# Opening a fused encoder step with three plain feed-forward tiles instead of four, and with token-wise sums of squares

## Chip, cores, metric

The kernel runs on one core of one Trainium2 chip. The metric is the device time of one execution in microseconds, given as the median of several runs. A profile is one further execution, recorded by the hardware profiler.

## What is computed

One inference step of an encoder trunk with two layers, for 512 prompt frames and 8 x 16 sample frames, 640 tokens in all, width 1024. Each layer has a half-step feed-forward block, a mixer (short convolution, banded attention, gates) and a second half-step feed-forward block. What matters here is the very first feed-forward block:

```python
def _rmsnorm(x, g):
    xf = x.astype(jnp.float32)
    y = xf * lax.rsqrt(jnp.mean(xf * xf, axis=-1, keepdims=True) + EPS)
    return y.astype(x.dtype) * g

def _swiglu(h, w_gu, w_down):
    gu = h @ w_gu
    g, u = jnp.split(gu, 2, axis=-1)
    return (jax.nn.silu(g) * u) @ w_down
...
xp = xp + 0.5 * _swiglu(_rmsnorm(xp, norm_ffn1[l]), w_ffn1_gu[l], w_ffn1_down[l])
```

The inner width is 2816, that is 22 tiles of 128 columns for the gate and 22 for the up projection.

## The kernel before

**Layout and precision.** Activations lie transposed: 128 channels on the partitions, 640 tokens along the row, eight such k-tiles `x[0..7]`, each in two halves of 320 tokens. Every operand of a matrix product is split into a high part (`hi`, a rounded copy made by ScalarE, `ACT`) and a low part (`lo`, source minus high part, made by VectorE, `DVE`). A product is the sum of three matmuls: high by high, high by low, low by high. Weights stream from HBM as slabs of 128x1024 (`raw`), and each slab is split the same way (`whi` at L305, `wlo` at L310).

**Plain tiles and tiles by seven.** A plain gate or up product of one 128-column tile takes 8 k-tiles x 3 x 2 halves = 48 matmuls of 320 columns. A pair of gate and up takes two such products, 96 matmuls. The alternative computes gate and up together by a seven-product scheme of the Strassen kind over halves of k (even and odd k-tiles), halves of tokens and the pair gate/up: seven blocks of 12 matmuls, 84 in all. The blocks are named by their left operand: X11, XT5, XN6, X21, XT7, X22, XT4, in the order of the first such tile. This scheme needs sums of x (`Expand`, with the pieces `xe` of an even row and `xo` of an odd row, held split as `xhi`/`xlo`, four pairs of rows), and sums of weights: four slabs per tile, made out of two raw slabs by VectorE additions at L249 (`s`, then `raw<-raw,raw` and `raw<-s,raw`).

**The opening (`opening`, before the first tile by seven).** The sums of x are not there yet when the kernel starts, so the first tiles of the block are plain. `FFNS["a0"]` says how many: 4. Their eight products `po` 0 to 7 alternate gate and up. They run on x times the gain only; the rms factor per token (`rho`) is applied afterwards, when a product is taken out of its bank. The two banks of `po` alternate, so product i+2 needs product i taken out. Sums of squares come from ScalarE squares (L571, L574), VectorE additions into `ssum`, a matmul with a column of ones (`nps`, L472), a square root on ScalarE, a reciprocal and a diagonal on VectorE, and two matmuls that spread the factor over the partitions (`nbc`, L595), which ScalarE copies into `rho` (L597). Then the first tile by seven is computed by `gate_up` with `first` set; its third block may start only when ScalarE has copied the first block's sum out of the same bank (`c1`, L761).

**Order.** In this part PE, DVE and ACT issue in the order of the code (`manual_schedule`), each engine its own queue. Where one instruction waits, everything behind it on that engine waits. SP issues the loads of x and the slabs, three slab buffers deep. After the opening come tile 4, and then, in turn, two down products (`pd`, taken into x at L1102) and one tile by seven.

## Time and profile before

| | before |
|---|---|
| median of 3 runs | 2496.51 us (2495.89 to 2498.94) |
| the profiled execution | 2496.66 us |
| its span from first to last instruction | 2494.7 us |
| PE, DVE, ACT busy | 99%, 85%, 58% of the span |
| PE matmuls | 17048 |
| moved by DMA | 308.10 MB |
| granted clock of TensorE | 0.998 |

In the rows below, a line begins with the start in microseconds from the span's start and its length, then engine, source line, operation, result and sources, the shape, how many were merged, and in brackets how long the engine had been idle and what ended that. In the chain rows stand start, length, engine and result. In the rows by stretch stand the stretch, its length, the busy time and count of PE, PE's weight loads, DVE, ACT and POOL, then granted clock, DMA share and GB/s. Lengths overlap slightly on one engine, so the price of an operation is better read from start to start.

### The profile page before, as it was taken

The page shows a single profiled execution, that of the slowest core. Times are in us where ns is not written, and L with a number is a line of the kernel's source. Part 1 is how long each engine was busy: PE and PEld are TensorE (multiplying, and loading weights), DVE is VectorE, ACT ScalarE, POOL GpSimd, SP SyncE. Part 2 cuts the span into 40 slices and gives each one's busy share as a digit, 9 for nine tenths or more (in the row PEclk, how much of TensorE's full clock was granted, in tenths as well). Part 3 has the DMA queues.
Part 4 walks back from the last instruction along what each step waited for, and adds up shares of the span by engine and source line. Part 5 has one row for each costly group of instructions (what it writes and reads, how often), then busy time and mean ns, then how long its engine had stood idle before and what let it go on. Part 6 is the DMA issues. An engine that isn't in the chain of part 4 may idle for free.

```text
span 2494.7 us, 43515 instructions
## 1 busy us (share of the span) xinstructions
PE 2478.1 (99%) x17048; PEld 2419.0 (97%) x17048; DVE 2119.2 (85%) x3322; ACT 1450.0 (58%) x2343; POOL 370.7 (15%) x445
## 2 busy tenths in 40 slices
PE   9999999999999999999999999999999999999998
PEld 8999999888999999999999999998899999999998
DVE  7888888878888899888798889888788888989887
ACT  7455556674666555555565555556646665555554
POOL 0011211211111011111001111221111110111111
PEclk9999999999999999999999999999999999999999
DMA  4245665335345344655435555643344553455554
GB/s 146 82 107 124 138 135 130 106 115 167 99 119 145 101 116 118 138 135 135 117 90 126 129 134 123 138 119 115 125 153 104 126 141 95 119 133 122 129 135 110
DMA packets 133261, 308.10 MB, mean 124 GB/s; under 512 B 12768, under 2 KB 76128, under 8 KB 133056
## 3 DMA queue, kind: packets, MB, share of 16 engines
q1 hardware_dynamic: 68976, 219.18, 27.3%
q0 software_dynamic: 63360, 85.50, 20.6%
q8 instruction: 133, 2.18, 0.4%
q10 hardware_dynamic: 720, 0.65, 0.1%
q14 instruction: 72, 0.59, 0.1%
HBM read 221.13 MB, written 7.94 MB: 92 GB/s over the span
## 4 chain that ended last, share of the span: by engine, by line
PE 94%; DVE 3%; ACT 2%; DMA 1%; issue 0%; SPq 0%; DVEq 0%; ACTq 0%
PE pab L395 12%; PE paa L395 11%; PE pcb L395 6%; PE pca L395 6%; PE daa L962 5%; PE dab L962 5%; PE po L372 4%; PE qa L395 4%; PE pbb L395 3%; PE pba L395 3%; PE dca L962 3%; PE dcb L962 3%; PE pda L372 2%; PE pv L1622 2%; PE ma_cv L395 2%; PE qc L395 2%
## 5 line engine op out<-in xcount | busy, mean ns | idle before, releaser
L310 DVE TENSOR_TENSOR wlo<-raw,whi 128x512 fp32r<-128x512 f32 (+1 forms) x583 | 598.6, 1030 | 236.1 <-ACT whi L305 230.6
L305 ACT CAST whi<-raw 128x512 fp32r<-128x512 f32 (+1 forms) x583 | 519.9, 897 | 348.0 <-PE pbb L395 44.6
L305 ACT CAST whi<-s 128x1024 fp32r<-128x1024 f32 (+1 forms) x164 | 153.6, 937 | 248.1 <-issue 107.8
L395 PE MATMUL pab<-xhib,whi 128*128 128x320 f32 x704 | 218.3, 310 | 0.4 <-DVE gb L249 0.4
L395 PE MATMUL pab<-xhib,wlo 128*128 128x320 f32 x704 | 217.4, 309 | 0.0
L395 PE MATMUL pab<-xlob,whi 128*128 128x320 f32 x704 | 217.4, 309 | 0.0
L395 PE MATMUL paa<-xhia,whi 128*128 128x320 f32 x640 | 198.0, 309 | 0.2 <-DVE ga L249 0.2
L395 PE MATMUL paa<-xloa,whi 128*128 128x320 f32 x640 | 197.6, 309 | 0.0
L395 PE MATMUL paa<-xhia,wlo 128*128 128x320 f32 x640 | 197.6, 309 | 0.0
L310 DVE TENSOR_TENSOR wlo<-s,whi 128x1024 fp32r<-128x1024 f32 (+1 forms) x164 | 176.6, 1077 | 10.4 <-ACT whi L305 10.4
L395 PEld LDWEIGHTS pab<-xhib,whi 128*128 128x128 f32 x704 | 132.2, 188 | 1.1 <-DVE gb L249 0.9
L395 PEld LDWEIGHTS pab<-xlob,whi 128*128 128x128 f32 x704 | 132.2, 188 | 0.2
L395 PEld LDWEIGHTS pab<-xhib,wlo 128*128 128x128 f32 x704 | 132.2, 188 | 0.0
L395 PEld LDWEIGHTS paa<-xhia,whi 128*128 128x128 f32 x640 | 120.2, 188 | 0.5 <-DVE ga L249 0.5
L395 PEld LDWEIGHTS paa<-xloa,whi 128*128 128x128 f32 x640 | 120.2, 188 | 0.1
L395 PEld LDWEIGHTS paa<-xhia,wlo 128*128 128x128 f32 x640 | 120.2, 188 | 0.0
L249 DVE TENSOR_TENSOR raw<-raw,raw 128x512 f32<-128x512 f32 x164 | 112.2, 684 | 1.8 <-DMA raw<-in_wst 0.2
L249 DVE TENSOR_TENSOR raw<-s,raw 128x512 f32<-128x512 f32 x164 | 112.3, 685 | 0.0
L395 PE MATMUL pcb<-xhib,whi 128*128 128x320 f32 x352 | 108.7, 309 | 0.0
L395 PE MATMUL pcb<-xlob,whi 128*128 128x320 f32 x352 | 108.7, 309 | 0.0
L395 PE MATMUL pcb<-xhib,wlo 128*128 128x320 f32 x352 | 108.7, 309 | 0.0
L986 POOL DMA_DIRECT2D x<-c_b x52 | 62.6, 1203 | 309.5 <-ACT c_b L979 134.5
(816 smaller groups left out, 8170.8 us busy)
## 6 DMA issues: line engine op xcount, KB each, us to landing
raw<-in_wst SPq DMA_DIRECT2D x375, 512.0 KB, 3.7
x<-c_b POOLq DMA_DIRECT2D x52, 320.0 KB, 5.1
x<-c_a POOLq DMA_DIRECT2D x50, 320.0 KB, 5.0
kc<-in_kcache SPq DMA_DIRECT2D x32, 256.0 KB, 4.1
vc<-in_vcache SPq DMA_DIRECT2D x16, 512.0 KB, 4.5
ub<-cbb POOLq DMA_DIRECT2D x42, 160.0 KB, 5.9
ua<-cba POOLq DMA_DIRECT2D x38, 160.0 KB, 5.4
x<-u_a POOLq DMA_DIRECT2D x18, 320.0 KB, 5.1
```

What stands on the lines that cost most here:

```text
L249: DVE.tensor_tensor(out=out, in0=a, in1=b, op=ALU.add)
L305: ACT.copy(hi[:, d], src[:, c])
L310: DVE.tensor_tensor(out=lo, in0=src, in1=hi.bitcast(F32), op=ALU.subtract)
L372: PE.matmul(ps[a] if isinstance(ps, list) else ps[:, a, :HT], w, x[:, a * HT : (a + 1) * HT], start=first and j == 0, stop=last and j == 2)
L395: PE.matmul(ps, a, b, start=start and kp == 0 and j == 0, stop=stop and kp == NP - 1 and j == 2, skip_group_check=True)
L962: PE.matmul(ps[u], w, y, start=start and i == 0 and j == 0, stop=i == 1 and j == 2, skip_group_check=True)
L986: POOL.dma_start(rows(r, cols), z, accum_op=ALU.add)
L1622: PE.matmul(pv[t], xx[:, t * P : (t + 1) * P], w[:, kk * AW : (kk + 1) * AW], start=c == 0 and kk == 0 and j == 0, stop=c == KT // 2 - 1 a ...
```

## The change

Three plain tiles instead of four, the fourth (tile 3) by seven, so the opening has six products. The first two products are computed side by side, k-tile by k-tile, and the first two slabs are loaded in alternating quarters. For odd rows the operand of the plain products is written where the seven-product scheme wants it, so `Expand.final` no longer casts and splits it a second time. The sums of squares come from a second copy of x laid out by tokens (`xtok`, 5 tiles of 128 tokens x 1024, 2.6 MB), loaded behind x: ScalarE squares each tile in place and sums along the row (`accum_out`). The VectorE additions and the matmul with ones are gone. The tokens lie in buffers that are free at that time.

```diff
-FFNS = {"a0": ((4, 4, 4, 4, 4, 2), 4), "b0": ((4, 4, 4, 4, 6), 0),
+FFNS = {"a0": ((4, 4, 4, 4, 4, 2), 3), "b0": ((4, 4, 4, 4, 6), 0),
...
         if k % 2 == 0:
             c = slice(k * P, (k + 2) * P)
-            SP.dma_start(raws[0][:, c], wst[0][:, c])
+            for n in range(2):
+                SP.dma_start(raws[n][:, c], wst[n][:, c])
...
                 self.flush()
-                ACT.copy(hi[:, 3:5], O[:, 3:5])
+                if whole:
+                    ACT.copy(hi[:, 3:5], O[:, 3:5])
...
-                self.late.append((lo[:, 3:5], O[:, 3:5], hi[:, 3:5]))
+                if whole:
+                    self.late.append((lo[:, 3:5], O[:, 3:5], hi[:, 3:5]))
...
+        ex.ps = fp.tile([P, NT], F32, name=f"sums{name}", bufs=1)
+        load(2)
+        for c in range(NT):
+            if c < 2:
+                z = fp.tile([P, D], F32, tag=("s65", "odd")[c], name=f"tok{name}_{c}", bufs=1)
...
+                SP.dma_start(t, xtok[c][:, a * D // 2 : (a + 1) * D // 2])
...
-        made = {2: (0, 1), 3: (2, 3), 4: (4,), 5: (5, 6), 6: (7,)}
+        made = {2: (2, 3), 3: (4,), 4: (5, 6), 5: (7,)}
...
-        at = {2: {4: begun}, 3: {1: lambda: ex.spread([att(f"nbc{name}_{a}")[:, :HT] for a in range(2)])}}
+        def square(c):
+            for z, total in toks[c]:
+                ACT.activation(z, z, AF.Square, accum_out=total)
+
+        at = {3: {5: lambda: ex.spread([att(f"nbc{name}_{a}")[:, :HT] for a in range(2)])}}
...
             if i == 1:
-                continue
+                ws = [[tiles.take() for _ in range(KT)]]
+                pair = quiet()
+                ws.append([tuple(z[:, k * P : (k + 1) * P] for z in pair) for k in range(KT)])
+                for ks in (*((k,) for k in range(KT - 2)), (KT - 2, KT - 1)):
+                    for p, w in zip(ps, ws):
+                        for k in ks:
+                            multiply(p, w[k], h[k], k == 0, k == KT - 1)
+                flush()
+                ex.final(0, False)
+                square(0)
+                out(0)
+                square(1)
+                ex.final(1, False, True)
+                out(1)
+                square(2)
+                ex.rest()
+                prep(len(ready))
+                flush()
+                for c in range(3, NT):
+                    square(c)
+                add(ex.ps[:, 2:], ex.ps[:, 2:], rest)
+                ex.root()
+                ex.diagonal()
```

What this does to the order is shown at three places. First PE at the start of the program. Before, product 0 (`poa_0`) alone:

```order
L372 MATMUL poa_0_159<-hhia_0_119,whi_117 128x320 x2
L372 MATMUL poa_0_159<-hloa_0_120,whi_117 128x320 x2
L372 MATMUL poa_0_159<-hhia_0_119,wlo_118 128x320 x2
L372 MATMUL poa_0_159<-hhia_1_125,whi_117 128x320 x2
L372 MATMUL poa_0_159<-hloa_1_126,whi_117 128x320 x2
```

Now, the same place on PE; `poa_1` is product 1, and the odd row's operand is `xhia`/`xloa`:

```order
L372 MATMUL poa_0_194<-hhia_0_148,whi_142 128x320 x2
L372 MATMUL poa_0_194<-hloa_0_149,whi_142 128x320 x2
L372 MATMUL poa_0_194<-hhia_0_148,wlo_143 128x320 x2
L372 MATMUL poa_1_195<-hhia_0_148,whi_144 128x320 x2
L372 MATMUL poa_1_195<-hloa_0_149,whi_144 128x320 x2
L372 MATMUL poa_1_195<-hhia_0_148,wlo_145 128x320 x2
L372 MATMUL poa_0_194<-xhia_0_146,whi_142 128x320 x2
```

Product 1's matmuls of a k-tile now follow product 0's of the same k-tile. Second, ACT between the end of product 0 and the square root (`nrmsa`), before; `sqa` are squares of x by channels, `whi` casts of slabs:

```order
L639 COPY ga_0_223<-poa_0_159 128x640
L574 ACTIVATE sqa_2_225<-x 128x640
L574 ACTIVATE sqa_3_228<-x 128x640
L574 ACTIVATE sqa_4_231<-x 128x640
L574 ACTIVATE sqa_5_235<-x 128x640
L574 ACTIVATE sqa_6_238<-x 128x640
L574 ACTIVATE sqa_7_241<-x 128x640
L305 CAST whi_247<-raw_245 128x1024
L305 CAST whi_302<-raw_300 128x1024
L585 ACT_TABLE_LOAD
L585 ACTIVATE nrmsa_113<-npsa_329,epst 128x5
```

And ACT now, on the second half of the way to the root; `toka` are token tiles, squared in place, `xoa` and `xhia` pieces of the first pair of rows:

```order
L677 COPY ua_0_310<-poa_1_195 128x640
L681 ACTIVATE toka_20_130,sumsa_122<-toka_20_130 128x512
L681 ACTIVATE toka_21_132,resta_125<-toka_21_132 128x512
L551 CAST xhia_0_146<-xoa_0_304 128x960
L305 CAST whi_317<-raw_315 128x1024
L681 ACTIVATE toka_30_134,sumsa_122<-toka_30_134 128x512
L681 ACTIVATE toka_31_136,resta_125<-toka_31_136 128x512
L681 ACTIVATE toka_40_138,sumsa_122<-toka_40_138 128x512
L681 ACTIVATE toka_41_140,resta_125<-toka_41_140 128x512
L594 ACT_TABLE_LOAD
L594 ACTIVATE nrmsa_118<-sumsa_122,epst 128x5
```

The root now stands directly behind the squares on the same engine, and the first pair's pieces have moved ahead of it. Third, DVE ahead of the first tile by seven, before; `xoa_3`/`xloa_3` belong to the last pair of rows, `s_8` and `raw_605` are the sums of that tile's weights, `ga_3` the gate of the last plain tile:

```order
L537 TENSOR_TENSOR xoa_3_662<-xoa_3_662,xea_3_597 128x320
L556 TENSOR_TENSOR xloa_3_599<-xoa_3_662,xhia_3_598 128x640
L556 TENSOR_TENSOR xloa_3_599<-xoa_3_662,xhia_3_598 128x960
L249 TENSOR_TENSOR s_8_675<-raw_673 128x512
L249 TENSOR_TENSOR s_8_675<-s_8_675,raw_605 128x512
L487 TENSOR_TENSOR ga_3_729<-poa_6_604,rhoa_116 128x640
L310 TENSOR_TENSOR wlo_679<-s_8_675,whi_678 128x1024
L249 TENSOR_TENSOR raw_605<-raw_605,raw_673 128x512
L249 TENSOR_TENSOR raw_605<-s_8_675,raw_605 128x512
```

And DVE now, at the corresponding place; `s_6` and `raw_471` are the weights of tile 3:

```order
L249 TENSOR_TENSOR s_6_543<-raw_541 128x512
L249 TENSOR_TENSOR s_6_543<-s_6_543,raw_471 128x512
L489 TENSOR_TENSOR ga_2_597<-poa_4_470,rhoa_121 128x640
L310 TENSOR_TENSOR wlo_547<-s_6_543,whi_546 128x1024
L565 TENSOR_TENSOR xloa_3_183<-xea_3_535,xhia_3_182 128x640
L543 SCALAR_TENSOR_TENSOR xoa_3_601<-xea_3_535,xoa_3_601 128x320
L543 SCALAR_TENSOR_TENSOR xoa_3_601<-xoa_3_601 128x320
L545 TENSOR_TENSOR xoa_3_601<-xoa_3_601,xea_3_535 128x320
L565 TENSOR_TENSOR xloa_3_183<-xoa_3_601,xhia_3_182 128x960
L249 TENSOR_TENSOR raw_471<-raw_471,raw_541 128x512
L249 TENSOR_TENSOR raw_471<-s_6_543,raw_471 128x512
```

The 640-wide split of the odd row is gone, and the last pair's pieces now stand between the first and the second sum of weights.

More of the change, by code (lines that the diff above doesn't have):

```diff
@@ L180, in trunk @@
 @with_exitstack
-def trunk(ctx: ExitStack, tc: tile.TileContext, xin, wst, small, pbias, samplebias, kcache, vcache,
+def trunk(ctx: ExitStack, tc: tile.TileContext, xin, xtok, wst, small, pbias, samplebias, kcache, vcache,
           yout, ko, vo, co):
@@ L417, in trunk @@
         if k == 0:
-            raws.append(wp.tile([P, CH], F32, tag="raw", name="raw0", bufs=3))
+            for n in range(2):
+                raws.append(wp.tile([P, CH], F32, tag="raw", name=f"raw{n}", bufs=3))
         if k % 2 == 0:
             c = slice(k * P, (k + 2) * P)
-            SP.dma_start(raws[0][:, c], wst[0][:, c])
+            for n in range(2):
+                SP.dma_start(raws[n][:, c], wst[n][:, c])
     def norm(pool, name, goff, ssum):
@@ L501, in __init__, with place, final @@
             self.known = False
-        def final(self, m, square=True):
+        def place(self, kp):
+            self.ops.append(tuple(self.fp.tile([P, 7, HT], F32R, name=f"x{t}{self.name}_{kp}", tag=f"x{t}{kp}")
+                                  for t in ("hi", "lo")))
+        def final(self, m, whole=True, hold=False):
+            square = whole
             kp, odd = divmod(m, 2)
@@ L509, in final @@
                 self.E = self.fp.tile([P, 3, HT], F32, name=f"xe{n}", tag="even", bufs=1)
-                hi = self.fp.tile([P, 7, HT], F32R, name=f"xhi{n}", tag=f"xhi{kp}")
-                lo = self.fp.tile([P, 7, HT], F32R, name=f"xlo{n}", tag=f"xlo{kp}")
-                self.ops.append((hi, lo))
+                if whole:
+                    self.place(kp)
             else:
@@ L537, in final @@
                 DVE.tensor_tensor(out=O[:, XT7], in0=O[:, 4], in1=E[:, 2], op=ALU.subtract)
-                self.late.append((lo[:, 3:5], O[:, 3:5], hi[:, 3:5]))
+                if whole:
+                    self.late.append((lo[:, 3:5], O[:, 3:5], hi[:, 3:5]))
                 self.flush()
@@ L547, in final @@
                 self.rest = rest
-                if not end:
+                if not (end or hold):
                     rest()
@@ L607, in opening @@
         ex = Expand(fp, name, goff)
+        ex.ps = fp.tile([P, NT], F32, name=f"sums{name}", bufs=1)
+        load(2)
+        toks = []
+        rest = fp.tile([P, NT], F32, name=f"rest{name}", bufs=1)[:, : NT - 2]
+        for c in range(NT):
+            if c < 2:
+                z = fp.tile([P, D], F32, tag=("s65", "odd")[c], name=f"tok{name}_{c}", bufs=1)
+                toks.append([(z, ex.ps[:, c : c + 1])])
+                SP.dma_start(z, xtok[c])
+                continue
+            toks.append([])
+            for a, (tag, z) in enumerate((("hhi", ex.ps[:, c : c + 1]), ("hlo", rest[:, c - 2 : c - 1]))):
+                t = hp.tile([P, T], F32, tag=tag, name=f"tok{name}_{c}{a}")[:, : D // 2]
+                toks[c].append((t, z))
+                SP.dma_start(t, xtok[c][:, a * D // 2 : (a + 1) * D // 2])
@@ L608, in opening @@
         h = []
-        whi, wlo = (wp.tile([P, CH], F32R, tag=f"w{t}", name=f"w{t}0", bufs=3) for t in ("hi", "lo"))
-        ready.append((whi, wlo))
+        for n_ in range(2):
+            ready.append(tuple(wp.tile([P, CH], F32R, tag=f"w{t}", name=f"w{t}{n_}", bufs=3) for t in ("hi", "lo")))
         for k in range(KT):
             g = sm[:, goff + k : goff + k + 1]
-            hi = hp.tile([P, T], F32R, tag="hhi", name=f"hhi{name}_{k}")
-            lo = hp.tile([P, T], F32R, tag="hlo", name=f"hlo{name}_{k}")
+            kp, odd = divmod(k, 2)
+            if odd:
+                hi, lo = (z[:, 3:5].rearrange("p a b -> p (a b)") for z in ex.ops[kp])
+            else:
+                ex.place(kp)
+                hi = hp.tile([P, T], F32R, tag="hhi", name=f"hhi{name}_{k}")
+                lo = hp.tile([P, T], F32R, tag="hlo", name=f"hlo{name}_{k}")
@@ L615, in opening @@
             ACT.activation(hi, x[k], AF.Copy, scale=g)
             c = slice(k * P, (k + 2) * P)
-            if k % 2 == 0:
-                ACT.copy(whi[:, c], raws[0][:, c])
+            if not odd:
+                for (whi, _), raw in zip(ready, raws):
+                    ACT.copy(whi[:, c], raw[:, c])
             DVE.scalar_tensor_tensor(out=lo, in0=x[k], scalar=g, in1=hi.bitcast(F32),
                                      op0=ALU.mult, op1=ALU.subtract)
-            if k % 2 == 0:
-                DVE.tensor_tensor(out=wlo[:, c], in0=raws[0][:, c], in1=whi[:, c].bitcast(F32),
-                                  op=ALU.subtract)
+            if not odd:
+                for (whi, wlo), raw in zip(ready, raws):
+                    DVE.tensor_tensor(out=wlo[:, c], in0=raw[:, c], in1=whi[:, c].bitcast(F32),
+                                      op=ALU.subtract)
@@ L624, in opening @@
             h.append((hi, lo))
-        flush()
-        made = {2: (0, 1), 3: (2, 3), 4: (4,), 5: (5, 6), 6: (7,)}
+        made = {2: (2, 3), 3: (4,), 4: (5, 6), 5: (7,)}
         us, gs, ps = [], [], []
@@ L647, in out @@
                 ACT.copy(halves(u), two(ps[i]))
-        def begun():
-            ex.total(att(f"nps{name}"))
-            ex.root()
-            ex.diagonal()
-        at = {2: {4: begun}, 3: {1: lambda: ex.spread([att(f"nbc{name}_{a}")[:, :HT] for a in range(2)])}}
+        def square(c):
+            for z, total in toks[c]:
+                ACT.activation(z, z, AF.Square, accum_out=total)
+        at = {3: {5: lambda: ex.spread([att(f"nbc{name}_{a}")[:, :HT] for a in range(2)])}}
         for i in range(2 * n):
             ps.append(acc(f"po{name}_{i}"))
-            product(ps[i], h, at.get(i, {}))
-            if i > 1:
-                out(i - 1)
             if i == 0:
-                for k in range(KT):
-                    ex.square(k)
-                    ex.add()
-                    if k == 1:
-                        out(0)
-                    if k == 4:
-                        flush()
-            if i == 1:
-                continue
+                continue
+            if i == 1:
+                ws = [[tiles.take() for _ in range(KT)]]
[21 more added lines that the diff above has]
+                ex.diagonal()
+            else:
+                product(ps[i], h, at.get(i, {}))
+                if i > 2:
+                    out(i - 1)
             if i == 3:
@@ L2082, in _layout @@
     vc = i["cache_v"].reshape(L, NB, 2, P, AW).transpose(0, 1, 3, 2, 4)
-    return {"xin": xin, "wst": _stream(i), "small": small, "pbias": pbias, "samplebias": sbias, "kcache": kc, "vcache": vc}
+    return {"xin": xin, "xtok": tok.reshape(NT, P, D), "wst": _stream(i), "small": small, "pbias": pbias, "samplebias": sbias, "kcache": kc, "vcache": vc}
 _OUTS = {
```

## The prediction

> **What bounds the kernel now.** I read the page first: busy times and the chain that ended last.

> ```profile
> PE 2478.1 (99%) x17048; PEld 2419.0 (97%) x17048; DVE 2119.2 (85%) x3322; ACT 1450.0 (58%) x2343; POOL 370.7 (15%) x445
> PE 94%; DVE 3%; ACT 2%; DMA 1%; issue 0%; SPq 0%; DVEq 0%; ACTq 0%
> ```

> TensorE is never free for long. A change confined to the opening is therefore read at one point: where the first down product (`pda`) starts. Behind it the order of work is the same in both kernels, and a shift there reaches the end unchanged. Next, the chain in order of time gives that point and the matmul work ahead of it.

> ```profile
> 16.29 10.23 PE poa L372 x68
> 26.52 1.01 PE npsa L472 x10
> ...
> 32.04 1.08 PE nbca L595 x4
> ...
> 70.96 1.76 PE paa L395 x12
> ...
> 79.76 7.04 PE pda L372 x48
> ```

> From 16.29 us PE runs without a stop. One matmul costs 7.04/48 = 0.147 us, a block of 12 costs 1.76, a plain product of 48 costs 7.04. Block 3 of the first by-seven tile (XN6, at 70.96) is followed by four more blocks to 79.76. Last, the busy times by stretch show how near the feeders are:

> ```profile
> 5.60:16.30 10.70, 10.24 (x53) 9.06 (x53) 9.21 (x13) 8.85 (x13) 0.00 (x0) 1.00 1.03 393
> 39.30:53.40 14.10, 14.10 (x98) 14.10 (x98) 13.76 (x21) 9.34 (x13) 0.00 (x0) 1.00 0.31 86
> 53.40:67.40 14.00, 14.00 (x97) 14.00 (x96) 12.07 (x17) 7.38 (x9) 0.00 (x0) 1.00 0.07 28
> ```

> During products 4 and 5 DVE is 98% busy, during 6 and 7 it is 86%. The change takes the 14 us of products 6 and 7 away, while nearly all of DVE's work in them must still precede the first by-seven tile. That is the heart of the case.

> **The change part by part: what PE gains.** Tile 3 by seven takes 84 matmuls where two plain products take 96: 12 x 0.147 = 1.76 us less. The column sums by matmul go: 1.01 less (the two spreading matmuls, 1.08, stay). The interleaving fills the stalls of the first product:

> ```profile
> 5.63 0.90 PE L372 MATMUL poa<-hhia,whi 128*128 128x320 f32 x2 [5.63 <-ACT whi L618]
> ...
> 9.02 0.46 PE L372 MATMUL poa<-hhia,whi 128*128 128x320 f32 x2
> ```

> The first 12 matmuls take 9.02 - 5.63 = 3.39 us, at half pace. In the changed order the other 84 of products 0 and 1 follow at 0.147 (12.32 us), so these products end at 21.3. Before, 24 matmuls of product 2 stand ahead of the sums at 26.52, so the two ended at 26.52 - 3.52 = 23.0. Gain 1.7. A pair of k-tiles needs about 2.4 us of ACT and of DVE against 3.5 of PE, so PE leads there, and the 0.5 MB of second weights ahead of the last x costs 1.3 us at the 393 GB/s above, which PE reaches too late to feel. Together 1.76 + 1.01 + 1.7 = 4.5 us: if the feeders kept up.

> **When rho is ready.** The rms factor rho now waits for ScalarE alone: all token squares, the table load and the root stand in one queue.

> ```profile
> 17.43 0.67 ACT L639 COPY ga<-poa 128x640 f32<-128x640 f32 x1
> ...
> 22.13 1.98 ACT L305 CAST whi<-raw 128x1024 fp32r<-128x1024 f32 x2
> ...
> 24.13 1.28 ACT L585 ACT_TABLE_LOAD   x1
> ...
> 27.57 0.27 ACT L585 ACTIVATE nrmsa<-npsa,epst 128x5 f32<-128x5 f32 x1 [2.16 <-PE npsa L472]
> ...
> 31.22 0.83 ACT L521 ACTIVATE xoa<-x,sm 128x640 f32<-128x640 f32 x1
> ...
> 33.55 1.00 ACT L542 CAST xhia<-xoa 128x960 fp32r<-128x960 f32 x1 [0.74 <-DVE xoa L537]
> ...
> 35.39 0.75 ACT L597 COPY rhoa<-nbca 128x320 f32<-128x320 f32 x2
> 36.16 1.28 ACT L599 ACT_TABLE_LOAD   x1
> 37.45 0.20 ACT L599 ACTIVATE early<-epst 128x1 f32<-128x1 f32 x1
> ```

> ```profile
> 496.14 0.71 ACT L1828 ACTIVATE s<-s,st 128x512 f32<-128x512 f32 x1
> 496.76 0.18 ACT L1828 ACTIVATION_READ_ACCUMULATOR s<-s,st 128x1 f32 x1
> ```

> An ACT operation starts about 0.1 us before the one ahead ends. No square with a sum exists before. The nearest rows are the cast (0.95 per 1024) and the accumulating exponential (its read adds 0.18, half of it overlapped). I take cast + 0.09: 1.04 per 1024, 0.61 per 512; bounds 0 and 0.18 on each of the seven still ahead of the root, so 0.6 us either way. Product 0's result is out at 21.3 - 1.76 + 0.3 = 19.9. Then: copy 0.57, square 1.04, odd row 0.85 (its buffer held that token), copy 0.57, two half squares 1.22, cast 960 0.9, cast of slab 3 0.95, four halves 2.44, table load 1.28, root 0.27: 10.1, so the reciprocal starts at 30.0.

> [...]

> ```profile
> 27.87 0.19 DVE L589 RECIPROCAL ninva<-nrmsa 128x5 f32<-128x5 f32 x1 [1.56 <-ACT nrmsa L585]
> 36.17 0.82 DVE L487 TENSOR_TENSOR ga<-poa,rhoa 128x640 f32<-128x640 f32 x1 [1.93 <-ACT rhoa L597]
> ```

> From reciprocal to first use of rho the same kinds of work stand as before, 36.17 - 27.87 = 8.3, plus 0.4 because the odd row waits for the 960-wide split of the pair before it. First use: 38.7 to 38.8. Product 4 would begin at 21.3 + 14.1 + 1.1 = 36.5, but its bank holds product 2, which that use evicts, ending at 39.6. New PE wait: 3.1 us (before, the eviction ended 2.3 us ahead of product 4).

> **VectorE from rho to the third split.** Block 3 of tile 3 accumulates into a bank that ScalarE must first copy out; that copy is queued behind the cast of the tile's third weight slab, and that cast waits for two VectorE additions. Everything on PE is queued behind. The prices:

> ```profile
> 53.11 0.82 DVE L556 TENSOR_TENSOR xloa<-xoa,xhia 128x640 fp32r<-128x640 f32 x1
> 54.98 0.49 DVE L527 TENSOR_TENSOR xea<-xea 128x320 f32<-128x320 f32 x1 [1.06 <-ACT xea L521]
> 55.39 1.15 DVE L556 TENSOR_TENSOR xloa<-xoa,xhia 128x960 fp32r<-128x960 f32 x1
> ...
> 59.19 0.82 DVE L556 TENSOR_TENSOR xloa<-xea,xhia 128x640 fp32r<-128x640 f32 x1
> 59.93 0.48 DVE L535 SCALAR_TENSOR_TENSOR xoa<-xea,xoa 128x320 f32<-128x320 f32 x1
> ...
> 61.26 0.82 DVE L556 TENSOR_TENSOR xloa<-xoa,xhia 128x640 fp32r<-128x640 f32 x1
> 62.41 1.16 DVE L556 TENSOR_TENSOR xloa<-xoa,xhia 128x960 fp32r<-128x960 f32 x1 [0.33 <-ACT xhia L542]
> 63.48 0.68 DVE L249 TENSOR_TENSOR s<-raw 128x512 f32<-128x512 f32 x1
> ...
> 64.81 0.82 DVE L487 TENSOR_TENSOR ga<-poa,rhoa 128x640 f32<-128x640 f32 x1
> 66.06 1.23 DVE L310 TENSOR_TENSOR wlo<-s,whi 128x1024 fp32r<-128x1024 f32 x1 [0.43 <-ACT whi L305]
> 67.20 0.69 DVE L249 TENSOR_TENSOR raw<-raw,raw 128x512 f32<-128x512 f32 x1
> 67.80 0.69 DVE L249 TENSOR_TENSOR raw<-s,raw 128x512 f32<-128x512 f32 x1
> ```

> Start to start: a 640-wide operation 0.74, a 1024 split 1.14, a 960 split 1.07, the three odd combinations 1.33, a difference 0.41, two sums of weights 1.33. From first use of rho, in the new order: six 640-wide operations of the gate and up tails 4.5 (with a dependence), two splits 2.3 (plus 0.15 for the first row's cast), difference 0.4, a 960 split 1.1: 8.4. Pair 2: split 0.74, combinations 1.33. Then ScalarE casts them and scales the next even row before VectorE goes on: 53.11 to 54.98, 1.87. The odd split removed by the change stood inside that gap and inside the next one (61.26 to 62.41, 1.15), so it saves nothing there. Difference and 960 split 1.48, sums 1.33, gate tail and cast 1.25, split 1.14: 17.5 so far. Pair 3: 0.74 + 1.33 + 1.15 + 1.07 = 4.3, then the two additions, ending 1.3 later: 23.2. So 38.8 + 23.2 = 62.0. Cast and copy follow:

> ```profile
> 68.58 1.05 ACT L305 CAST whi<-raw 128x1024 fp32r<-128x1024 f32 x1 [1.91 <-DVE raw L249]
> 69.54 0.42 ACT L761 COPY ua<-paa 128x320 f32<-128x320 f32 x1
> ```

> 0.1 + 0.96 + 0.42 brings block 3 to 63.5 (before, the copy ended at 69.96, 1.0 ahead of PE). Then five blocks 8.8, tile 4's seven blocks 12.3, and about 0.3 for its second slab, which VectorE, with 5.6 us of work behind tile 3's sixth block, finishes that much too late. The first down product starts at 84.9 to 85.0, against 79.76: **5.2 us later**. Read the other way: 4.5 gained, 9.7 waited: 3.1 at product 4, 6.3 in tile 3 (PE is there at 39.6 + 14.1 = 53.7; some 2 in block 1, on pair 3's first split, ended at 57.1, and 4 ahead of block 3), 0.3 in tile 4.

> At no cost: tile 4's product through POOL's accumulating DMA, since its result is wanted two blocks later; tile 3's two extra casts on ScalarE, 52 to 66% busy here, apart from the one on the path above.

> The profiled run took 2496.66 us (span 2494.7, 1.96 around it), 0.15 above the median 2496.51. 2496.66 + 5.2 = 2501.9. By the bounds on the squares and half a microsecond in the handoffs, this case's own range is 2500.5 to 2503.5. About 0.2%, 5 us, is what a measurement of this kernel can tell from no change; the sum lies just beyond it.

> **The rivals.** *The feeders keep up* (chance 0.11): PE gains its 4.5 us, 2492.2, faster. For it: VectorE idles 12.07 of 14 in the last stretch. Against it: it decides only if the additions end by PE's earliest arrival at block 3, 36.5 + 14.1 + 3.5 = 54.1, less 1.5 for cast and copy: 9.4 us earlier than summed.

> *VectorE's handoffs shrink* (0.14): the gaps of 1.87, 1.15 and the 0.4 cast wait exist only if ScalarE is late there. With all three gone 3.4 come back: 2498.5, no difference.

> *PE falls back to half pace after a long wait* (0.13): the wait before block 3 is about 4 us, and the only PE wait of that length in the trace, the start, is followed by 12 matmuls at half pace, 3.39 instead of 1.76. Repeated there, 1.6 more: 2503.5. Half pace after the first two waits would be swallowed by the next. [...]

> *rho later still* (0.12): tokens share the queue with weights. Slab 3 lands after 7.46 MB (x and the tokens 2.6 each, four slabs of 0.52, the small tensor); even counted from 5.6 us, at 393 GB/s, that is 24.6, and its cast stands at 25.1. [...]

> **How the numbers follow.** My case has 0.50, of it 0.30 beyond the bound and 0.20 within; with the two slower rivals 0.55 slower, with the shrunk handoffs 0.34 same, 0.11 faster. The range takes in the handoff rival and the slower two with the upper bound of the squares: 2497.5 to 2505.

> **What would show it.** Right: a PE wait of about 3 us near 36 to 40 on VectorE's eviction with rho; a second near 55 to 57 on a split of pair 3; a third of about 4 us ending near 63.5 on ScalarE's copy; `pda` starting near 85; VectorE nearly full from 39 to 62. Wrong: `pda` before 80, or a stretch behind it in which the shift changes; matmuls 0.28 apart after the third wait would mean the half-pace rival.

## The result, and the profile after

The changed kernel takes 2505.56 us (median of 6 runs, 2505.09 to 2507.09) against 2496.48 (6 runs, 2495.89 to 2498.94): 9.1 us more, ratio 1.0035, 95% interval 1.0026 to 1.0045. The forecast was 2501.9 with a range up to 2505.0. The side was right, and the loss about 1.7 times the 5.2 us of the sum. The profiled execution took 2507.09, the longest of the six; the others lie between 2505.09 and 2505.71.

The page after, busy times and the shares of the chain that ended last:

```profile
PE 2480.2 (99%) x17026; PEld 2421.2 (97%) x17026; DVE 2116.0 (84%) x3324; ACT 1450.6 (58%) x2356; POOL 371.6 (15%) x446
PE 93%; DVE 4%; ACT 3%; issue 0%; DMA 0%; DVEq 0%; ACTq 0%
```

Nothing there tells of the change: PE is 99% busy in a slower kernel, and matmuls at half pace count as busy (14 of them fill the whole 3.40 us of the stretch from 66.70 below). The chain in order of time tells more (start, length, engine, result, line):

```profile
6.14 15.38 PE poa L372 x84
...
21.54 0.70 ACT ga L669
...
31.90 0.20 DVE ninva L598
...
39.92 0.65 ACT rhoa L606 x2
...
65.26 3.57 PE paa L395 x12
68.83 2.47 PE pba L395 x12
71.29 1.76 PE paa L395 x12
...
89.37 7.04 PE pda L372 x48
```

Before, PE entered this chain at 16.29 and stayed in it up to `pda` at 79.76. Now the chain runs through ScalarE and VectorE from 21.54 to 65.26, and `pda` starts 9.6 later. Block 3 of tile 3 (XN6, at 65.26) takes 3.57 and block 4 (X21) 2.47, where a block took 1.76. What TensorE waited for up to 100 us (in total, times, longest):

```profile
PE poa L372 <- ACT whi L648: 6.1, 1, 6.1
PE paa L395 <- ACT ua L807: 3.9, 1, 3.9
PE poa L372 <- DVE ga L489: 3.0, 1, 3.0
PE paa L395 <- DVE xloa L565: 0.2, 1, 0.2
```

These are the start and the three waits that the prediction named: product 4 on VectorE's eviction, a split of pair 3 in block 1, ScalarE's copy ahead of block 3. The rows behind the prediction's prices: ScalarE first, then VectorE's first use of rho and the second of the two additions for which block 3's cast and copy wait:

```profile
28.32 0.62 ACT L681 ACTIVATE toka<-toka 128x512 f32<-128x512 f32 x1
28.84 0.19 ACT L681 ACTIVATION_READ_ACCUMULATOR toka<-toka 128x1 f32 x1
28.93 0.62 ACT L681 ACTIVATE toka<-toka 128x512 f32<-128x512 f32 x1
...
30.27 1.28 ACT L594 ACT_TABLE_LOAD   x1
31.57 0.30 ACT L594 ACTIVATE nrmsa<-sumsa,epst 128x5 f32<-128x5 f32 x1
...
40.60 0.82 DVE L489 TENSOR_TENSOR ga<-poa,rhoa 128x640 f32<-128x640 f32 x1 [2.66 <-ACT rhoa L606]
...
63.06 0.68 DVE L249 TENSOR_TENSOR raw<-s,raw 128x512 f32<-128x512 f32 x1
```

A half square costs 28.93 - 28.32 = 0.61, the table load 1.30 to the root's start, from reciprocal to first use 8.70, from first use to the end of the additions 63.74 - 40.60 = 23.1: the prediction's 0.61, 1.28, 8.7 and 23.2. All of these held; the chain only began later, and something was added at its end.

Both differences are the pace of TensorE. Stretches of 3.4 us (length, PE, PEld, DVE, ACT and POOL busy with counts, granted clock, DMA share, GB/s):

```profile
5.30:8.70 3.40, 2.56 (x9) 2.44 (x10) 2.54 (x5) 2.92 (x6) 0.00 (x0) 1.00 1.03 374
8.70:12.10 3.40, 3.40 (x15) 3.40 (x14) 3.28 (x6) 3.03 (x7) 0.00 (x0) 1.00 0.97 351
36.00:39.40 3.40, 2.43 (x17) 2.17 (x15) 1.75 (x4) 1.91 (x3) 0.00 (x0) 1.00 0.25 99
39.40:42.80 3.40, 1.32 (x9) 1.32 (x10) 2.20 (x3) 3.37 (x7) 0.00 (x0) 1.00 0.01 2
42.80:46.20 3.40, 3.40 (x15) 3.40 (x15) 3.34 (x5) 2.84 (x5) 0.00 (x0) 0.52 0.34 89
59.90:63.30 3.40, 1.48 (x11) 1.21 (x9) 2.34 (x5) 0.99 (x1) 0.00 (x0) 1.00 0.00 0
63.30:66.70 3.40, 1.44 (x5) 1.44 (x6) 3.37 (x5) 2.70 (x5) 0.00 (x0) 0.52 0.00 0
66.70:70.10 3.40, 3.40 (x14) 3.40 (x14) 1.24 (x2) 1.59 (x5) 0.00 (x0) 0.50 0.45 154
70.10:73.50 3.40, 3.40 (x25) 3.40 (x24) 2.17 (x4) 1.38 (x2) 0.00 (x0) 0.98 0.03 5
```

A full stretch holds 25 matmuls at full pace (last row). The stretches from 8.70, 42.80 and 66.70 hold 14 or 15. Half pace in the opening thus lasted from 6.14 to about 12.2, where before it had ended near 9.0; and it came back twice, behind the first and the third wait.

One more wait, of 1.6 us in the second layer's mixer, is in this execution and not in that of before: a weight slab landed late.

```profile
1996.14 0.69 DVE L249 TENSOR_TENSOR raw<-raw,raw 128x512 f32<-128x512 f32 x1 [1.52 <-DMA raw<-in_wst]
```

It is about as long as the 1.5 us by which this execution exceeds the median; the executions that took less were not profiled.

### The profile page after: what moved, and what is told of

It reads as the page before. It is cut to its first block, busy times and chain, and to the rows that moved or that the text cites. A ratio compares the mean times of both kernels' runs of the same rounds, so it can differ in the third digit from the quotient of the medians.

```text
span 2505.3 us, 43496 instructions
## 1 busy us (share of the span) xinstructions
PE 2480.2 (99%) x17026; PEld 2421.2 (97%) x17026; DVE 2116.0 (84%) x3324; ACT 1450.6 (58%) x2356; POOL 371.6 (15%) x446
## 4 chain that ended last, share of the span: by engine, by line
PE 93%; DVE 4%; ACT 3%; issue 0%; DMA 0%; DVEq 0%; ACTq 0%
PE pab L395 12%; PE paa L395 11%; PE pcb L395 6%; PE pca L395 6%; PE dab L1008 5%; PE daa L1008 5%; PE po L372 4%; PE qa L395 4%; PE pbb L395 3%; PE pba L395 3%; PE dcb L1008 3%; PE dca L1008 3%; PE pda L372 2%; PE pv L1668 2%; PE ma_cv L395 2%; PE qc L395 2%
## 5 line engine op out<-in xcount | busy, mean ns | idle before, releaser
L310 DVE TENSOR_TENSOR wlo<-raw,whi 128x512 fp32r<-128x512 f32 (+1 forms) x583 | 597.9, 1029 | 239.3 <-ACT whi L305 234.9
L305 ACT CAST whi<-raw 128x512 fp32r<-128x512 f32 (+1 forms) x583 | 519.5, 896 | 347.7 <-PE pbb L395 44.3
L305 ACT CAST whi<-s 128x1024 fp32r<-128x1024 f32 (+1 forms) x165 | 154.5, 936 | 254.2 <-issue 108.1
L395 PE MATMUL pab<-xhib,whi 128*128 128x320 f32 x704 | 218.1, 310 | 0.4 <-DVE gb L249 0.4
L395 PE MATMUL pab<-xlob,whi 128*128 128x320 f32 x704 | 217.2, 309 | 0.0
L395 PE MATMUL pab<-xhib,wlo 128*128 128x320 f32 x704 | 217.2, 309 | 0.0
L395 PE MATMUL paa<-xhia,whi 128*128 128x320 f32 x656 | 203.9, 311 | 4.1 <-ACT ua L807 3.9
L395 PE MATMUL paa<-xloa,whi 128*128 128x320 f32 x656 | 203.3, 310 | 0.2 <-DVE xloa L565 0.2
L395 PE MATMUL paa<-xhia,wlo 128*128 128x320 f32 x656 | 203.3, 310 | 0.1
L310 DVE TENSOR_TENSOR wlo<-s,whi 128x1024 fp32r<-128x1024 f32 (+1 forms) x165 | 177.8, 1077 | 10.4 <-ACT whi L305 10.3
L395 PEld LDWEIGHTS pab<-xhib,whi 128*128 128x128 f32 x704 | 132.1, 188 | 1.1 <-DVE gb L249 0.9
L395 PEld LDWEIGHTS pab<-xlob,whi 128*128 128x128 f32 x704 | 132.1, 188 | 0.2
L395 PEld LDWEIGHTS pab<-xhib,wlo 128*128 128x128 f32 x704 | 132.1, 188 | 0.0
L395 PEld LDWEIGHTS paa<-xhia,whi 128*128 128x128 f32 x656 | 123.7, 189 | 4.8 <-ACT ua L807 4.1
L395 PEld LDWEIGHTS paa<-xloa,whi 128*128 128x128 f32 x656 | 123.8, 189 | 0.6 <-DVE xloa L565 0.5
L395 PEld LDWEIGHTS paa<-xhia,wlo 128*128 128x128 f32 x656 | 123.8, 189 | 0.3 <-DVE wlo L310 0.3
L249 DVE TENSOR_TENSOR raw<-raw,raw 128x512 f32<-128x512 f32 x165 | 112.8, 684 | 3.5 <-DMA raw<-in_wst 1.9
L249 DVE TENSOR_TENSOR raw<-s,raw 128x512 f32<-128x512 f32 x165 | 112.9, 684 | 0.0
L395 PE MATMUL pcb<-xhib,whi 128*128 128x320 f32 x352 | 108.7, 309 | 0.0
L395 PE MATMUL pcb<-xlob,whi 128*128 128x320 f32 x352 | 108.6, 309 | 0.0
L395 PE MATMUL pcb<-xhib,wlo 128*128 128x320 f32 x352 | 108.6, 309 | 0.0
```

Source lines behind the costliest of these rows:

```text
L249: DVE.tensor_tensor(out=out, in0=a, in1=b, op=ALU.add)
L305: ACT.copy(hi[:, d], src[:, c])
L310: DVE.tensor_tensor(out=lo, in0=src, in1=hi.bitcast(F32), op=ALU.subtract)
L395: PE.matmul(ps, a, b, start=start and kp == 0 and j == 0, stop=stop and kp == NP - 1 and j == 2, skip_group_check=True)
```

## The experiments

All times are medians; the ratio is to the kernel before, run on the same chip beside it.

### 1. Is it the pace? (e2_fill, e1_warm, e5_dense_warm_fill)

Fill the third wait with matmuls that nobody needs:

```diff
+                spare, kept = acc(f"fill{n}")[:, 0, :HT], ex.ops[0][0][:, XT5]
+                for _ in range(20):
+                    PE.matmul(spare, s1[0][:, :P], kept, start=True, stop=True)
                 mul(pa, s1, 0, XN6, every, False, True)
```

> The changed kernel plus 20 matmuls of 320 columns (2.9 us) between tile 3's second block and its third, into a bank that nothing reads, so that TensorE works through most of the third wait (3.88 us). Clock theory: block 3 still starts at 65.26, but its matmuls are 0.147 apart instead of 0.267, pda starts 2.2 us earlier, near 87.2, and the time is 2503.3. Rival: the 0.267 comes from the blocks themselves (weights or banks), not from the pause; spacing and time stay as they are, 2505.5.

Measured 2503.38 (2502.34 to 2503.80, 9 runs), ratio 1.0024 (1.0014 to 1.0034): 2.2 us less than the changed kernel, and within a tenth of what the clock theory said (2503.3). The matmuls and the stretches of the same place:

```profile
61.19 3.10 PE L826 MATMUL filla<-xhia,whi 128*128 128x320 f32 x20
65.25 0.41 PE L395 MATMUL paa<-xhia,whi 128*128 128x320 f32 x1 [0.96 <-ACT ua L807]
65.50 0.31 PE L395 MATMUL paa<-xloa,whi 128*128 128x320 f32 x1
```

```profile
63.30:66.70 3.40, 2.44 (x17) 2.18 (x16) 3.37 (x5) 2.71 (x5) 0.00 (x0) 1.00 0.02 5
66.70:70.10 3.40, 3.40 (x25) 3.40 (x25) 2.26 (x4) 2.96 (x6) 0.00 (x0) 1.00 0.45 154
```

Block 3 starts at 65.25, where it started at 65.26 in the changed kernel, yet the clock reads 1.00, and 25 matmuls fit where there were 14. So the half pace behind the third wait is a cost of its own, 2.2 us on top of the wait.

The same idea for the opening, first try:

```diff
+        cold, one = att(f"warm{name}")[:, :P], ones.bitcast(F32R)
+        for _ in range(42):
+            PE.matmul(cold, one, one, start=True, stop=True)
```

> The changed kernel plus 42 matmuls of 128 columns on a tile of ones, from about 1.3 us on, into a bank that nothing reads; they end before the first product's operands are there. Clock theory (the opening came 1.6 us later than summed because TensorE stayed at half pace until 12.1 us, not until about 8.8 as before): products 0 and 1 run at 0.147 a matmul from the start, product 0's copy starts near 19.9 instead of 21.54, rho and all that hangs on it come 1.6 us earlier, and the time falls to 2503 to 2504. Feeder theory (the opening is late because ScalarE, VectorE and the loads deliver the pieces later): the copy stays at 21.5 and the time at 2505.5.

Measured 2507.70 (2507.08 to 2508.19, 5 runs), ratio 1.0043 (1.0030 to 1.0055): slower, and neither theory was tested.

```profile
1.14 9.22 PE L634 MATMUL warma<-ones 128*128 128x128 f32 x42 [1.14 <-POOL ones L404]
...
11.33 0.73 PE L372 MATMUL poa<-hhia,wlo 128*128 128x320 f32 x2
...
12.40 0.33 PE L372 MATMUL poa<-hloa,whi 128*128 128x320 f32 x1
```

The 42 took 0.22 each, twice what I had reckoned, and the first product began 4 us late. And though PE was busy from 1.14 on, the pace stayed halved to 12.4. Why is not shown. The second try uses fewer and wider matmuls, 19 of 320 columns, on a tile that VectorE does not need yet, together with the fill:

```diff
+    cold = tmp("cold")[:, :HT]
+    POOL.memset(cold, 1.0)
...
+            PE.matmul(unused, cold[:, :P].bitcast(F32R), cold.bitcast(F32R), start=True, stop=True)
```

> The filled kernel (2503.38) plus 19 matmuls of 320 columns on a tile of ones from about 1.2 us until just ahead of the first product, into a bank that nothing reads. [...] Clock theory: half pace ends during or right behind these matmuls, products 0 and 1 run at 0.147, product 0's copy comes near 19.9 instead of 21.54, all that hangs on rho 1.65 earlier, pda near 85.3: 2501.7. Feeder theory: what comes late in the opening is the pieces; 2503.4, the copy at 21.5.

Measured 2502.14 (2501.72 to 2503.76, 11 runs), ratio 1.0024 (1.0014 to 1.0033). The pace is full from the first product on: two matmuls take 0.46, or 0.56 where one of them waits a little, against 0.73 at half pace:

```profile
1.16 5.29 PE L636 MATMUL warma<-cold 128*128 128x320 f32 x19 [1.16 <-POOL cold L403]
6.29 0.46 PE L372 MATMUL poa<-hhia,whi 128*128 128x320 f32 x2
6.76 0.56 PE L372 MATMUL poa<-hloa,whi 128*128 128x320 f32 x2
...
19.36 1.06 ACT L686 ACTIVATE toka<-toka 128x1024 f32<-128x1024 f32 x1
...
20.41 0.67 ACT L674 COPY ga<-poa 128x640 f32<-128x640 f32 x1
```

The gain is 1.2 us, not 1.65: product 0 was out of PE earlier, but its copy started at 20.41 instead of 19.9, because ScalarE was still squaring token 0. Without half pace in the opening and behind the third wait the kernel stands at 2502.1, close to the prediction's 2501.9. That agreement is partly luck. The sum held 12 matmuls at half pace (1.6 us more than at full pace), which this run does not have; and it held neither the first matmul's later start (6.29, not 5.63) nor this square ahead of the copy.

The warm-up ahead of the kernel before (e11):

> The kernel before, with the same 19 matmuls ahead of its first product. Clock theory: its first product waits for pieces anyway and the slow start costs it little; pda within 0.3 us of 79.6, 2496.3. Rival: it gains as much as the changed kernel, 1.2 or more, 2495.2; then the slow start is no disadvantage of the change.

Measured 2496.20 (2495.24 to 2497.11, 11 runs), ratio 0.9997 (0.9988 to 1.0006): no difference that can be told, and `pda` 0.4 earlier (79.34). In the two profiles, then, the slow start cost the old order little, and its first product does wait for pieces (0.4 us for a weight's low part in both). But the profile of before is one in which half pace ended early, at 9.0, and the interval of the times also holds a gain of 1.2, so the rival is not excluded.

### 2. Which part of the change costs? (e7_four_plain, e8_three_only)

```diff
-FFNS = {"a0": ((4, 4, 4, 4, 4, 2), 3), ...
+FFNS = {"a0": ((4, 4, 4, 4, 4, 2), 4), ...
```

> The changed kernel with four plain tiles again: interleaved opening, token squares and in-place splits stay, tile 3 is plain. Chain theory: rho is as late as in the changed kernel, product 4 waits 3.1 and half pace behind it costs 1.5, but VectorE then has products 6 and 7 to catch up and the first tile by seven does not wait for the third slab: its block 3 starts near 74.7 instead of 70.96, pda near 83.4, 2500.3. Rival 1, the late opening alone makes the loss: 2505 or more. Rival 2, the opening costs nothing once VectorE has room: 2497 or less.

Measured 2499.26 (2498.69 to 2500.18, 11 runs), ratio 1.0011 (1.0002 to 1.0020): 2.7 over before (forecast 3.8). Product 4 still waits 3.1 on rho; there is no wait at the tile by seven. That wait, and where `pda` starts:

```profile
PE poa L372 <- DVE ga L489: 3.1, 1, 3.1
...
83.45 7.04 PE pda L372 x48
```

The other half alone, in the kernel before:

```diff
-FFNS = {"a0": ((4, 4, 4, 4, 4, 2), 4), ...
+FFNS = {"a0": ((4, 4, 4, 4, 4, 2), 3), ...
-        made = {2: (0, 1), 3: (2, 3), 4: (4,), 5: (5, 6), 6: (7,)}
+        made = {2: (0, 1), 3: (2, 3), 4: (4, 5), 5: (6, 7)}
```

> The kernel before with three plain tiles and nothing else of the change; rows 0 and 1 are made in product 2, then two rows in each product. rho is used from 36.2 as before. Chain theory: VectorE's additions, less some 4.5 us of work for products 6 and 7, end near 64.0 (68.5 before), cast and copy follow, block 3 starts near 65.5 after a wait of about 8.6; pda 87.0, with the half pace behind such a wait 88.6 to 89.5: 2504 to 2506.5, that is, the tile by seven alone costs nearly as much as the whole change. Rival: without the late rho the seven-product tile is free and gains its 1.76: 2494.8.

Measured 2508.15 (2506.77 to 2509.53, 5 runs), ratio 1.0045 (1.0031 to 1.0059): 11.6 over before.

```profile
64.78 3.29 PE paa L395 x12
...
87.91 7.04 PE pda L372 x48
...
PE pda L372 <- DVE x L1102: 2.3, 1, 2.3
```

Block 3 and `pda` came near the forecast (65.5; 87.0, or 88.6 with half pace), though after three waits of 2.8, 0.5 and 2.4 us and not one of 8.6. The time passed the forecast. In the profiled run a later down product waits 2.3 us on VectorE, once, up to 435.2 (last row), and behind it 14 matmuls at half pace take 1.5 more; together that is about the 3.9 by which the end was delayed more than `pda`. So the tile by seven is what costs: 8.2 at `pda` and 11.6 in the time alone, even with rho on time, and 6.3 on top of the new opening (2505.56 - 2499.26). Why the two parts together cost less than their sum is not shown: the token squares and the splits in place take work from VectorE, but the waits of the two parts also overlap.

### 3. Is the chain through rho the bound? (e3_rho_early, e6_root_table_first, e4_copy_first)

Copies of rho ahead of the cast of row 3:

```diff
+        def known():
+            ex.spread([att(f"nbc{name}_{a}")[:, :HT] for a in range(2)])
+            ex.rest()
+        at = {3: {5: known}}
...
-                ex.final(m, False)
+                ex.final(m, False, m == 3)
```

> The changed kernel with ScalarE's copies of rho ahead of the cast of row 3's three combinations, for which ScalarE had to wait until 37.98. Chain theory: the first use of rho moves from 40.60 to about 38.1, product 4's wait shrinks from 3.05 to about 0.5, block 3 of tile 3 starts 2.5 us earlier, near 62.8, and the time falls by 2.5, to 2503.0; where the half pace after that wait then lasts less long, by up to 0.7 more. Rival: rho is not what sets the third wait, because VectorE waits for ScalarE's casts of rows 5 to 7 anyway: block 3 stays within 0.5 us of 65.3 and the time at 2505.

Measured 2504.94 (2503.94 to 2507.07, 5 runs), ratio 1.0033 (1.0020 to 1.0045).

```profile
37.72 0.82 DVE L489 TENSOR_TENSOR ga<-poa,rhoa 128x640 f32<-128x640 f32 x1 [0.16 <-ACT rhoa L606]
...
42.10 0.49 DVE L534 TENSOR_TENSOR xea<-xea 128x320 f32<-128x320 f32 x1 [0.96 <-ACT xea L528]
```

rho was used 2.9 earlier (0.4 of it because the opening's half pace ended sooner in this run) and product 4 waited 0.8 (forecast 0.5). One microsecond was lost at once, in a new wait of VectorE (42.10): row 4's scaling on ScalarE now stands behind the Silu table's load, row 3's cast and two Silus. TensorE, which came earlier, now waited 2.6 in block 1; half pace began behind that wait, at 58.7, and after a further wait of 3.3 went on through block 3 and most of block 4. Block 3 came 2.0 earlier, at 63.26. Of the 2.5 forecast the profiled pair shows 1.8 at `pda`; the medians differ by 0.6 with 2 to 3 us of spread, so in the time the gain is not shown.

The root's table loaded while ScalarE has nothing to do:

```diff
-        ACT.copy(early, epst)
+        ACT.activation(early, epst, AF.Sqrt)
```

> The changed kernel with the table of the square root loaded at the start, where ScalarE waits for data, by making the first small instruction a square root; the load of 1.28 ahead of the root (30.27) is gone, the same table also serves squares and copies. Chain theory: root, reciprocal and everything queued behind them 1.28 earlier, first use of rho 39.3 instead of 40.6, product 4's wait 1.8 instead of 3.05, block 3 near 64.0: 2504.3. Rival: what sets rho's copies is not the root but VectorE's and ScalarE's work on rows 2 and 3 in front of them, or the spreading matmuls' place on TensorE (34.55): 2505.5.

Measured 2505.78 (2503.92 to 2508.50, 5 runs), ratio 1.0037 (1.0024 to 1.0050): no gain that can be told, with the widest spread of all. In the profiled run (2504.34) the load of 1.28 is gone, from product 0's copy to the first use of rho it is 38.48 - 20.50 = 18.0 instead of 19.1, and product 4 waits 2.0. The mechanism is there; its worth in the time stays open.

The third slab's cast behind the copy that block 3 needs:

```diff
         ahead()
-        begin()
         out(2 * n - 1)
```

> The changed kernel with the cast of tile 3's third slab queued on ScalarE behind the copy of the first block's sum instead of ahead of it. Chain theory: block 3 starts right behind block 2, near 61.3, without the wait of 3.88 and without the half pace behind it; the third slab itself is not earlier, so that block 5 (XT7) waits some 1.5 us for its split; pda starts about 4 us earlier, near 85.3, and the time is 2501.5 (2500.5 to 2503). Rival: what is late is the slab, whoever waits first: block 5 takes over the whole wait and the time stays above 2504.5.

Measured 2503.56 (2502.49 to 2504.69, 8 runs), ratio 1.0027 (1.0017 to 1.0037).

```profile
61.06 0.41 PE L395 MATMUL paa<-xhia,whi 128*128 128x320 f32 x1 [0.37 <-ACT ua L806]
...
66.76 0.42 PE L395 MATMUL paa<-xhia,whi 128*128 128x320 f32 x1 [1.91 <-ACT ua L825]
```

Block 3 started behind block 2 and half pace did not return. Block 5 (XT7) then waited 1.91, on ScalarE's copy `u2` (L825), which stands behind the third slab's cast and three other casts and copies. `pda` started at 85.1 in the profiled run, as forecast, though 0.7 of that came from an opening whose half pace ended sooner; the median gained 2.0 of the 4 and lies above the range told (2500.5 to 2503).

### 4. Can the change be made to pay? (e9_rebuilt, e10_rebuilt_cold, e12_changed_again)

The warm-up, the early table, rho's early copies and the later cast together (not the fill), with token 3 squared by VectorE and all squares and the root ahead of row 1's cast:

```diff
+        def other(c):
+            for z, total in toks[c]:
+                DVE.tensor_tensor_reduce(out=z, in0=z, in1=z, scale=1.0, scalar=0.0, op0=ALU.mult,
+                                         op1=ALU.add, accum_out=total)
...
+        at = {3: {1: known}}
...
+        made = {2: (2, 3), 3: (4, 5), 4: (6,), 5: (7,)}
```

> The changed kernel with everything that was found late set earlier: 19 dense matmuls before the first product; the root's table loaded at the start; token 3 squared and summed by VectorE while it is idle; all squares, root and reciprocal ahead of the cast of row 1's combinations and of the fourth slab; rho's copies in product 3 ahead of row 3's cast; the eviction of product 2 with rho directly behind them; rows 4 and 5 in product 3, row 6 in product 4; the third slab's additions ahead of the last split, its cast behind the copy of the first block's sum. Chain theory: rho is first used near 34 instead of 40.6, product 4 does not wait, no wait reaches 2 us and so TensorE keeps its pace; pda near 77 to 78.5 (79.6 before): 2494 to 2495.5. Rival: VectorE's work up to the third slab simply does not fit in six products, wherever it is put; pda 80 or later, 2497 or more.

Measured 2495.65 (2493.85 to 2498.33, 11 runs), ratio 0.9995 (0.9986 to 1.0004). The waits of TensorE up to 85 us, and `pda`:

```profile
PE warma L637 <- POOL cold L403: 1.2, 1, 1.2
PE paa L395 <- ACT ua L841: 0.8, 1, 0.8
PE poa L372 <- DVE ua L491: 0.7, 1, 0.7
PE poa L372 <- ACT whi L654: 0.2, 1, 0.2
```

```profile
77.77 7.04 PE pda L372 x48
```

rho is used from 34.47, no wait reaches 1 us once the products run, and `pda` starts at 77.77, 2.0 before that of the old kernel and inside the forecast. VectorE's work does fit. The kernel is 10.6 us faster than the changed one beside it (2506.22) and its median 1.35 below that of before, but the interval holds 1: that it beats the old kernel is not shown. The median lies 0.15 above the 2494 to 2495.5 told.

> The same without the 19 matmuls ahead of the first product. Clock theory: products 0 and 1 run at half pace until some point between 9.5 and 12.5 us, which puts rho and pda 1 to 1.5 us later: 2495 to 2497, and with more spread from run to run. Rival: with the later work put earlier, the opening's delay is absorbed by TensorE's slack; same as the warm one.

Measured 2496.77 (2495.22 to 2499.02, 11 runs), ratio 0.9999 (0.9990 to 1.0007); half pace up to 12.1, `pda` 1.1 later: the clock theory's amount, though the medians alone would not tell it. The greater spread that I expected is not there (3.8 us against 4.5).

> The changed kernel as it is, beside the others. Clock theory: the half pace of the opening ends at another point of this execution than 12.1 us, and product 0's copy moves with it, half a microsecond for each microsecond; the one behind the third wait is there again. Median 2505 to 2506. Rival: the end of the half pace is fixed by the work, 12.1 again.

Measured 2506.22 (2504.61 to 2507.49, 5 runs), ratio 1.0038 (1.0025 to 1.0050). Half pace ended near 12.3, as in the first profile, so here my expectation missed. It does move, though: the same opening ended it near 10.6 in e3 and e4, 9.6 in e6 and 11.6 in e7, and at 12.2 in e2.

## Why the prediction was right and wrong

- **Bound and reading point: right.** In the profiled runs the shift at `pda` and the shift of the end agree within 1.2 us, but for e8 (3.9) and e10 (1.9). Behind `pda` stand e8's wait on a down product with its half pace, and waits in the second layer's mixer, up to 2.3 us in some executions (e10, e12); in both profiles of the changed kernel a weight slab lands late there (1.52 and 1.88). Why it does stays open.
- **The opening: the first failed step.** "The other 84 of products 0 and 1 follow at 0.147 (12.32 us), so these products end at 21.3" took the length of half pace as a number of matmuls, 12, as before. It ended at 12.2 us instead of 9.0, after 22 matmuls (6.11 us), and the products ended at 23.1, so the 1.7 that the interleaving was to gain came to nothing (23.0 before). The length is no fixed price: counted from the first matmul, half pace lasted 3.4 us in the profile of before, 3.5 in e6 and 6.1 in the changed kernel and in e12. The prediction had one profile, which lies at the short end of these. "PE leads there" was right, and so the delay went whole into product 0's copy (21.54, not 19.9) and into rho. With a first matmul 0.5 later (6.14, not 5.63; ScalarE's first operands landed that much later, at 4.97 instead of 4.46) that made rho 1.8 late; the pace alone is worth 1.2 us by e5.
- **When rho is ready: right from the copy on.** From the copy to the first use 19.1 were measured and 18.9 summed; squares, read, table load (1.30 against 1.28) and the 8.7 behind the reciprocal are in the rows above.
- **VectorE from rho to the third split: right.** 23.1 against 23.2, wait at product 4 3.05 against 3.1, ahead of block 3 3.88 against about 4. The 2 us in block 1 shrank to 0.23 because half pace behind product 4's wait used up 1.5 of them, which the prediction had said such a stretch would do.
- **Half pace behind the third wait: the second failed step.** It stood among the rivals at 0.13 and 1.6 us, as if it excluded the sum or could be left out of it. It is a consequence of the wait that the sum itself contained, and cost 2.2 (e2).
- **The rest:** 5.2 + 1.2 + 2.2 = 8.6 of the 9.1. The first matmul's 0.5 would fill the gap, but no run takes it alone, and half a microsecond is within the spread of the runs. In the profiled run, at `pda`, it is 5.2, rho's 1.8 and the 2.5 that blocks 3 and 4 took above 3.5: 9.5 of 9.6.
- **The range** took the two slow rivals one at a time. Both came true together, half pace in full and rho 1.8 later, though from the pace and the later start: 2501.9 + 1.6 + 1.8 = 2505.3 would have been the prediction's own price for that. A rho made later by late slabs, or by more at the table than its load, which the range's upper end took in, no run shows: in the changed kernel ScalarE waits for no load between 21.54 and the root, and the root starts 1.30 behind the start of its table's load of 1.28.
- **Feeders keep up:** false for the change as it stands, but e9 shows that the order decides it, not VectorE's amount of work, which is larger there by token 3's squares.

## What to carry to other kernels

Where a change makes TensorE wait for a few microseconds (here 3.05 and 3.88, with 3.4 and 4.8 us at half pace behind them), price the wait and the slow matmuls behind it as one item, and say which later wait swallows them; behind the last wait nothing does. The opening that starved TensorE less gained less than its matmuls' count said (products 0 and 1 ended at 23.1 against 23.0, where 1.7 had been summed): without a warm-up the first 3.4 to 6.1 us of matmuls ran at half pace in every profile here, and 19 useless matmuls of 320 columns in the idle time ahead cost nothing there (2496.20, ratio 0.9997, in e11). Take such a length from more than one profile. And before work is taken from the engine that leads, count what its feeders must still do in the time that is left.
